# Block two of a feed-forward layer goes from a mix of eight and seven products to seven throughout, its weight sums supplied in another way

## The chip, the cores and the metric

The kernel runs on one core of one Trainium2 chip. The metric is device time in microseconds (us) of one launch; the time before is the median of three runs. The profile is that of one execution. Its times count from the first instruction of the span. PE is the matrix engine (PEld its weight loads), DVE the vector engine, ACT the scalar engine, POOL the GpSimd, and SP the engine whose queue issues most loads. Each engine runs its instructions in the order written and waits for others by semaphores.

## The reference

One decoder layer for 256 tokens of width 2048: a normalisation, one input projection, two groups of attention heads, an output projection, and then the feed-forward part, which alone is touched here:

```python
h = x + jnp.concatenate([gla_out, nsa_out], axis=-1) @ w_out
m = rms_norm(h, ffn_norm_g)
return h + (jax.nn.silu(m @ w_gate) * (m @ w_up)) @ w_down
```

`w_gate` and `w_up` are 2048 x 5632, `w_down` is 5632 x 2048, all float32.

## The kernel before

**Precision.** A float32 operand is kept as two parts: `hi`, a rounded copy in the matmul's input type, written by ACT (L661), and `lo`, what is left, `x - hi`, written by DVE (L662). One product of two operands is three matmuls: hi by hi, hi by lo, lo by hi.

**Blocks and pairs.** The 5632 columns are cut into eleven blocks of 512 (`f` = 0 to 10 in the code; "block one" to "block eleven" here, so block two is `f = 1`). In each block `gate_up` works through the 16 row tiles of the weights in eight pairs of two. Of a pair, the weights are four tiles of 128 x 512 (two of gate, two of up), and the tokens are two tiles of 128. Done plainly, a pair is eight products, 24 matmuls. Done in seven products, it is 21 matmuls, with four sums of the pair's weights and four sums of its tokens. The token sums are made once per pair (`pair_forms`); those of pairs 6 and 7 are made late (`late_forms`, during block two). `FIRST7` names the pairs that are done in seven in blocks one and two; from block three on all are.

**Where the weight sums come from.** There are three ways:
- *DVE*: one 128x1024 add and two 128x512 adds (L1229 to L1231).
- *DRAM sums* (`SUMS`): the four sums are made much earlier, in the attention part, by SP loads, DVE adds and POOL stores (`sum_rows`), kept in DRAM, and fetched by two POOL transfers of 512 KB (`fetch_sums`, L1172); the pair's own load is then 768 KB in place of 1 MB.
- *adding pair* (`HALVES`): two POOL transfers and a third that adds in flight make the first two sums in memory (`fetch_half`, L1182 to L1184); DVE makes the other two with two 128x512 adds. Its own load too is 768 KB.

In all of them the three plain tiles that are used (128x1536) and the four sums (two times 128x1024) are split by ACT and DVE into `ftwo` tiles, which a pair takes two of; a plain pair takes one of 128x2048. There are four `ftwo` tiles, four `fraw` tiles for the loads, and three `fsum` tiles, which hold weight sums and also the block's results on their way through the activation.

**After a block.** When the last seven-product pair is through, five operations (L1256 to L1260) put the product banks together; L1271 to L1275 add, apply the SiLU and multiply. `turn_act` then transposes the two result tiles on PE (L215), and splits them. `down` multiplies them with `w_down`: four chunks of 24 matmuls (L297), whose banks ACT seeds with the sum so far (L1310) and empties afterwards (L1322). `down` of a block stands behind the next block's pairs. In blocks three and later `turn_act` runs while the next block begins, in bank 8, which only plain pairs use otherwise; for block one it runs at the end of block two, in banks 1 and 5, since block two has plain pairs and needs bank 8.

**Order.** Instructions are put in order on each engine by a scheduler when the kernel is built. Loads are issued as soon as the tile that they fill is free.

Of the kernel before, what the change touches and what calls it, by code (L numbers as in the profile page):

```python
# [22 lines left out]
NFB = DFF // FB  # L23
# [14 lines left out]
def kernel(  # L38
# [989 lines left out]
    PAIRS7, FIRST7 = tuple(range(8)), {0: (0, 2, 4), 1: (0, 2, 3, 4, 5)}  # L1028
# [3 lines left out]
    HALVES = {f: (2, 6) if f < 8 else (2, 4, 6) for f in range(2, NFB)}  # L1032
# [4 lines left out]
    ORDER1 = (0,1,2,6,3,4,5,7)  # L1037
# [61 lines left out]
    SUMS = {f: (4, 7) if f < 8 else (7,) for f in range(2, NFB)}  # L1099
    SUMS[1] = (2, 3, 4, 5)  # L1100
# [87 lines left out]
    def gate_up(fb):  # L1188
# [12 lines left out]
        order, sevens = (ORDER0, ORDER1, ORDER)[min(fb, 2)], FIRST7.get(fb, PAIRS7)  # L1201
# [5 lines left out]
        if fb > 1:  # L1207
            urgent.append(turn_act(fb - 1, (8, 8)))
        for at, pair in enumerate(order):
            if fb > 1 and pair not in sevens:  # L1210
                drain(urgent)
# [42 lines left out]
            if pair == last7:  # L1254
                (q1, q7u), (u, q5u), (q57u, _) = ((t[:, 0], t[:, 1]) for t in (fw["sum"]([2, 512]) for _ in range(3)))
                act(q1, banks[1], AF.Copy)  # L1256
                TT(u, banks[6], q1, ALU.add)  # L1257
                TT(q5u, banks[5], u, ALU.subtract)
                TT(q7u, banks[7], u, ALU.add)
                TT(q57u, banks[5], q7u, ALU.subtract)  # L1260
                if fb == 1:
                    urgent.append(turn_act(0, (1, 5)))
                if fb:
                    seed(0, DOWN[min(fb - 1, 1)])
# [15 lines left out]
    def turn_act(fb, qs):  # L1280
# [4 lines left out]
        for t in range(NT):  # L1285
            ts = slice(t * P, (t + 1) * P)
            p = banks[qs[t]]
# [18 lines left out]
    DOWN = ((6, 7), (2, 3), (6, 7), (4, 8)), ((1, 6), (7, 5), (2, 3), (4, 1))  # L1306

    def seed(n, qs):
        for t in range(NT):
            last["seed", n] = nc.scalar.copy(banks[qs[n][t]], h_sb[n][:, t, :])  # L1310

    def down(f):
        ah, al = acts.pop(f)
        qs = DOWN[min(f, 1)]
        for n in range(4):
            bs = [banks[q] for q in qs[n]]
            ws = parts_of(load4([(w_down[0], 4 * f, 4, n * 512)]), last["seed", 0] if n == 2 and f else None)
            if n < 3 and (f or n != 1):
                seed(n + 1, qs)
# [3 lines left out]
            if n == 0 and not f:  # L1323
                seed(2, qs)
# [99 lines left out]
    for f in range(NFB):  # L1424
# [3 lines left out]
        if f:  # L1428
            drain(urgent)
            if f == NFB - 1:  # L1430
                urgent.append(turn_act(f, (8, 8)))
            drive([down(f - 1)], 3)
# [32 lines left out]
```

## Time and profile before

| | |
|---|---|
| median of three runs | 1095.1 us (1094.86 to 1095.49) |
| the profiled execution | 1095.91 us, its span 1094.2 us |
| busy share of the span | PE 99%, PEld 82%, DVE 90%, ACT 70%, POOL 12% |
| granted PE clock | 1.00 throughout |
| block one and two (`gate_up`) | 409.4 to 493.99 us; block two begins at 453.36 |
| `down` of block one | 493.99 to 516.41 us |
| block three, `down` of block two | 516.41 to 555.78, to 577.54 us |

The borders are the starts of the first matmuls, found by counting the matmuls of the trace along the program's order. The feed-forward part is 685 us of the span. A row of the windows view shows, for a stretch of time, how long each engine was busy and with how many instructions.

### The profile page before, as it was taken

Reading aid. Unit: us, or ns where it says so; the run is one execution under the profiler, and the core shown is the slowest. Engines: PE = TensorE matmul, PEld = TensorE weight load, DVE = VectorE, ACT = ScalarE, POOL = GpSimd, SP = SyncE. Lnnn points to the kernel's source line nnn. Section 1 sums busy time; section 2 is a strip of 40 time slices with the busy share of each in tenths; the row PEclk is TensorE's granted clock in tenths of the full one; section 3 lists DMA queues with packets and bytes.
Section 4 is the critical chain, followed back from the end, with each engine's and each line's share of the span. In section 5 each row is a group of like instructions: output and inputs, shape, how many; then the busy total and the mean of one; then the engine's idle time right before and its main releaser. Section 6 shows DMA issues by size and latency. Waiting matters only on the chain.

```text
span 1094.2 us, 14835 instructions
## 1 busy us (share of the span) xinstructions
PE 1088.2 (99%) x5256; PEld 895.3 (82%) x5256; DVE 988.4 (90%) x1316; ACT 764.7 (70%) x1060; POOL 129.2 (12%) x213
## 2 busy tenths in 40 slices
PE   9999999999999999999999999999999999999998
PEld 8888888987878877888888888888888887888877
DVE  6768879987799888997999999999999999999997
ACT  7745557555687586677686967777686877777695
POOL 4100001032110100010101011010101011110100
PEclk9999999999999999999999999999999999999999
DMA  7999978468876947696787969787797869788862
GB/s 278 357 356 350 398 251 295 166 232 287 308 274 252 342 153 287 216 336 208 250 278 221 299 200 302 246 266 236 261 288 236 280 207 288 227 279 255 247 231 78
DMA packets 135272, 287.76 MB, mean 263 GB/s; under 512 B 8135, under 2 KB 10219, under 8 KB 135197
## 3 DMA queue, kind: packets, MB, share of 16 engines
q1 hardware_dynamic: 112844, 218.17, 57.4%
q0 software_dynamic: 21744, 68.17, 20.4%
q8 instruction: 41, 0.67, 0.2%
q10 hardware_dynamic: 608, 0.47, 0.1%
q14 instruction: 35, 0.28, 0.1%
HBM read 263.71 MB, written 23.07 MB: 262 GB/s over the span
## 4 chain that ended last, share of the span: by engine, by line
PE 85%; DVE 6%; issue 3%; ACT 2%; DMA 2%; POOL 1%; SPq 0%; DVEq 0%; POOLq 0%; ACTq 0%
PE bank L297 41%; PE bank L1194 37%; PE bank L215 3%; PE bank L1339 2%; DVE lo L145 2%; PE bank L977 1%; DMA fraw<-in_w_up_dram 1%; DMA g<-in_w_up_dram 1%; POOL sm L218 1%; DMA sums<-g 1%; ACT g L912 1%; DVE ftwo L662 0%; DVE g L1115 0%; ACT hi L144 0%; PE bank L899 0%
## 5 line engine op out<-in xcount | busy, mean ns | idle before, releaser
L1194 PE MATMUL bank<-ftwo,g 128*128 128x512 f32 x1824 | 427.1, 393 | 0.5 <-ACT ftwo L661 0.2
L1194 PEld LDWEIGHTS bank<-ftwo,g 128*128 128x128 f32 x1824 | 337.2, 188 | 77.5 <-ACT ftwo L661 3.2
L297 PE MATMUL bank<-hi,g 128*128 128x512 f32 (+1 forms) x1088 | 320.9, 376 | 0.4 <-ACT g L912 0.4
L662 DVE TENSOR_TENSOR ftwo<-fraw,ftwo 128x1536 fp32r<-128x1536 f32 (+1 forms) x130 | 253.0, 1952 | 4.7 <-ACT ftwo L661 4.7
L661 ACT ACTIVATE ftwo<-fraw 128x1536 fp32r<-128x1536 f32 (+1 forms) x130 | 212.5, 1641 | 17.5 <-PE bank L1194 14.4
L297 PE MATMUL bank<-ftwo,g 128*128 128x512 f32 x960 | 221.6, 391 | 0.0
L297 PEld LDWEIGHTS bank<-hi,g 128*128 128x128 f32 x1088 | 191.5, 188 | 31.0 <-issue 1.0
L297 PEld LDWEIGHTS bank<-ftwo,g 128*128 128x128 f32 x960 | 179.3, 188 | 39.5 <-ACT bank L1310 1.2
L297 PE MATMUL bank<-lo,g 128*128 128x512 f32 (+3 forms) x544 | 193.0, 375 | 0.1
L144 ACT ACTIVATE hi<-raw 128x1024 fp32r<-128x1024 f32 (+3 forms) x124 | 130.5, 1059 | 82.8 <-PE bank L297 56.0
L145 DVE TENSOR_TENSOR lo<-raw,hi 128x1024 fp32r<-128x1024 f32 (+3 forms) x124 | 150.2, 1219 | 30.3 <-ACT hi L144 29.7
L661 ACT ACTIVATE ftwo<-fsum 128x1024 fp32r<-128x1024 f32 x118 | 121.9, 1054 | 70.6 <-DVE fsum L1229 53.6
L662 DVE TENSOR_TENSOR ftwo<-fsum,ftwo 128x1024 fp32r<-128x1024 f32 x118 | 142.0, 1221 | 13.7 <-ACT ftwo L661 13.7
L297 PEld LDWEIGHTS bank<-lo,g 128*128 128x128 f32 x544 | 98.2, 189 | 14.5 <-DVE lo L145 0.3
L661 ACT ACTIVATE ftwo<-g 128x1024 fp32r<-128x1024 f32 x46 | 48.7, 1059 | 35.8 <-PE bank L1194 23.3
L1322 ACT COPY g<-bank 128x512 f32<-128x512 f32 x80 | 45.6, 583 | 27.8 <-PE bank L297 26.4
L662 DVE TENSOR_TENSOR ftwo<-g,ftwo 128x1024 fp32r<-128x1024 f32 x46 | 56.2, 1221 | 2.2 <-ACT ftwo L661 2.2
L1119 POOL DMA_DIRECT2D sums<-g x40 | 21.8, 545 | 260.1 <-DVE g L1115 206.3
L1310 ACT COPY bank<-g 128x512 f32<-128x512 f32 x80 | 45.1, 589 | 7.6 <-DVE fsum L1257 6.2
L1229 DVE TENSOR_TENSOR fsum<-fraw 128x1024 f32<-128x1024 f32 x36 | 44.0, 1223 | 0.1
L215 PE MATMUL bank<-ident,g 128*128 128x128 f32 (+3 forms) x232 | 42.6, 277 | 0.6 <-ACT g L912 0.5
L1231 DVE TENSOR_TENSOR fsum<-fsum,fraw 128x512 f32<-128x512 f32 x60 | 41.4, 689 | 1.0
(251 smaller groups left out, 951.8 us busy)
## 6 DMA issues: line engine op xcount, KB each, us to landing
fraw<-in_w_gate_dram SPq DMA_DIRECT2D x86, 512.0 KB, 4.4
fraw<-in_w_down_dram SPq DMA_DIRECT2D x42, 1024.0 KB, 6.8
raw<-in_w_in_dram SPq DMA_DIRECT2D x36, 1024.0 KB, 6.1
fraw<-in_w_up_dram SPq DMA_DIRECT2D x45, 512.0 KB, 5.4
sums<-g POOLq DMA_DIRECT2D x40, 512.0 KB, 6.6
raw<-in_w_out_dram SPq DMA_DIRECT2D x16, 1024.0 KB, 8.5
g<-in_w_up_dram POOLq DMA_DIRECT2D x21, 512.0 KB, 7.6
fraw<-in_w_up_dram SPq DMA_DIRECT2D x41, 256.0 KB, 4.3
```

The source lines that it names most:

```text
L144: act(h[:, i:i + n], r[:, k + i:k + i + n], AF.Copy)
L145: last["d"] = TT(o[:, i:i + n], r[:, k + i:k + i + n], f32(h[:, i:i + n]), ALU.subtract)
L215: return nc.tensor.transpose(o, i, ident[:n, :n])
L297: last["mm"] = mm(bk[t], a[:, k, t * P:(t + 1) * P], ws[k][m][:, off:off + w], start=(first_ and k == 0 and i == 0), stop=(end and k == 3 ...
L661: act(hi, ps, AF.Copy)
L662: last["d"] = TT(lo, ps, f32(hi), ALU.subtract)
L1194: mm(banks[q], x, m, start=todo[q] == total[q], stop=todo[q] == 1)
L1229: TT(s1, r[:, 1:3], r[:, 3:4].to_broadcast([P, 2, 512]), ALU.add)
L1231: TT(s2[:, 1], s2[:, 0], r[:, 0], ALU.add)
L1310: last["seed", n] = nc.scalar.copy(banks[qs[n][t]], h_sb[n][:, t, :])
L1322: nc.scalar.copy(h_sb[n][:, t, :], bs[t])
L1339: mm(bk, u, m, start=(first and i == 0), stop=(end and i == 2), skip_group_check=onto)
```

## The change

Block two is done in seven products throughout: `FIRST7` loses its entry for it, and the order of its pairs becomes 0 to 7. Its DRAM sums are now those of the pairs 1, 3, 4, 6 and 7 (they were 2, 3, 4 and 5); the pairs 0, 2 and 5 have their sums made by DVE (before: pair 0 alone, while 1, 6 and 7 were plain and needed none). Block three (`f = 2`) gives up its DRAM sums of pair 4, which becomes a third adding pair, so that the number of stored sums stays at twenty pairs. Since bank 8 is now free in block two, `turn_act` of block one moves from the end of block two to its beginning, and `down` of block one takes its banks in the order that the later blocks have.

```diff
-    PAIRS7, FIRST7 = tuple(range(8)), {0: (0, 2, 4), 1: (0, 2, 3, 4, 5)}
+    PAIRS7, FIRST7 = tuple(range(8)), {0: (0, 2, 4)}
-    HALVES = {f: (2, 6) if f < 8 else (2, 4, 6) for f in range(2, NFB)}
+    HALVES = {f: (2, 6) if 2 < f < 8 else (2, 4, 6) for f in range(2, NFB)}
-    ORDER1 = (0,1,2,6,3,4,5,7)
-    SUMS = {f: (4, 7) if f < 8 else (7,) for f in range(2, NFB)}
-    SUMS[1] = (2, 3, 4, 5)
+    SUMS = {f: (4, 7) if 2 < f < 8 else (7,) for f in range(2, NFB)}
+    SUMS[1] = (1, 3, 4, 6, 7)
-        order, sevens = (ORDER0, ORDER1, ORDER)[min(fb, 2)], FIRST7.get(fb, PAIRS7)
+        order, sevens = (ORDER0, ORDER)[min(fb, 1)], FIRST7.get(fb, PAIRS7)
-        if fb > 1:
-            urgent.append(turn_act(fb - 1, (8, 8)))
+        if fb:
+            urgent.append(turn_act(fb - 1))
-                if fb == 1:
-                    urgent.append(turn_act(0, (1, 5)))
                 if fb:
-                    seed(0, DOWN[min(fb - 1, 1)])
+                    seed(0)
-    DOWN = ((6, 7), (2, 3), (6, 7), (4, 8)), ((1, 6), (7, 5), (2, 3), (4, 1))
+    DOWN = (1, 6), (7, 5), (2, 3), (4, 1)
```

**DVE, the last pairs of block two.** `fraw` is a load, `ftwo` a split tile, `fsum` and `g` hold sums. Before, pairs 4 and 5 (DRAM sums), then pair 7 (plain, 128x2048), then the first chunk of `down`:

```order
L662 TENSOR_TENSOR ftwo_4876<-fraw_4873,ftwo_4876 128x1536
L662 TENSOR_TENSOR ftwo_4888<-g_873_4833,ftwo_4888 128x1024
L662 TENSOR_TENSOR ftwo_4888<-fsum_4834,ftwo_4888 128x1024
L662 TENSOR_TENSOR ftwo_4908<-fraw_4905,ftwo_4908 128x1536
L662 TENSOR_TENSOR ftwo_4920<-g_878_4869,ftwo_4920 128x1024
L662 TENSOR_TENSOR ftwo_4920<-fsum_4870,ftwo_4920 128x1024
L662 TENSOR_TENSOR ftwo_4950<-fraw_4947,ftwo_4950 128x2048
L662 TENSOR_TENSOR ftwo_5001<-fraw_4999,ftwo_5001 128x2048
```

Now the end of pair 5 (sums by DVE), then pairs 6 and 7 (DRAM sums), then the first chunk of `down`:

```order
L1226 TENSOR_TENSOR g_888_4902<-fraw_4896 128x1024
L1227 TENSOR_TENSOR fsum_4903<-g_888_4902,fraw_4896 128x512
L1228 TENSOR_TENSOR fsum_4903<-fsum_4903,fraw_4896 128x512
L662 TENSOR_TENSOR ftwo_4916<-g_888_4902,ftwo_4916 128x1024
L662 TENSOR_TENSOR ftwo_4940<-fraw_4937,ftwo_4940 128x1536
L662 TENSOR_TENSOR ftwo_4916<-fsum_4903,ftwo_4916 128x1024
L662 TENSOR_TENSOR ftwo_4952<-g_884_4892,ftwo_4952 128x1024
L662 TENSOR_TENSOR ftwo_4952<-fsum_4893,ftwo_4952 128x1024
L662 TENSOR_TENSOR ftwo_4972<-fraw_4969,ftwo_4972 128x1536
L662 TENSOR_TENSOR ftwo_4975<-g_891_4933,ftwo_4975 128x1024
L662 TENSOR_TENSOR ftwo_4975<-fsum_4934,ftwo_4975 128x1024
L662 TENSOR_TENSOR ftwo_5020<-fraw_5018,ftwo_5020 128x2048
```

The last pair, for which one operation stood, now has three, and pair 5 has its three adds more. From the split of pair 0's load to the split of pair 7's last tile, DVE has 42 instructions before and 56 now.

**PE, the end of block two.** Before, pair 7 plain, with half of block one's transposes (L215) among it, and then `down` (L297):

```order
L1194 MATMUL bank_4386<-ftwo_4950,g_801_4337 128x512 x2
L1194 MATMUL bank_4386<-ftwo_4950,g_802_4338 128x512
L215 MATMUL bank_4464<-ident,fsum_4597 128x128 x2
L1194 MATMUL bank_4398<-ftwo_4950,g_801_4337 128x512 x2
L1194 MATMUL bank_4398<-ftwo_4950,g_802_4338 128x512
L297 MATMUL bank_4487<-ftwo_5001,g_891_4968 128x512 x2
```

Now pair 7 in seven products, from the first use of its third and fourth sums (bank_4487) on:

```order
L1193 MATMUL bank_4483<-ftwo_4975,g_882_4866 128x512 x3
L1193 MATMUL bank_4487<-ftwo_4975,g_882_4866 128x512 x2
L1193 MATMUL bank_4350<-ftwo_4972,g_801_4337 128x512 x2
L1193 MATMUL bank_4350<-ftwo_4972,g_802_4338 128x512
L1193 MATMUL bank_4369<-ftwo_4972,g_882_4866 128x512 x3
L1193 MATMUL bank_4386<-ftwo_4975,g_801_4337 128x512 x2
L1193 MATMUL bank_4386<-ftwo_4975,g_802_4338 128x512
L297 MATMUL bank_4464<-ftwo_5020,g_860_4713 128x512 x2
```

The two matmuls into bank_4487 need what DVE writes last for pair 7; with them 11 matmuls are left to the block's end. Block two has 168 matmuls now, and had 177; its transposes are all of block one's eight, and were four.

**POOL, the fetches for block two.** The stored tiles are named by block and pair (`sums_1_4` is `f = 1`, pair 4; two per pair). Before:

```order
L1172 DMA g_858_4715<-sums_1_2_749 128x1024 [waits DMASW2_49,PE_49]
L1172 DMA fsum_4716<-sums_1_2_750 128x1024 [waits DMASW3_49,DMASW1_49,DVE_49]
L1172 DMA fsum_4800<-sums_1_3_836 128x1024 [waits DMASW4_49,DVE_49]
L1172 DMA fsum_4834<-sums_1_4_927 128x1024 [waits DMASW5_49,DMASW3_49,DVE_49]
L1172 DMA g_869_4799<-sums_1_3_835 128x1024 [waits DMASW6_49]
L1172 DMA g_873_4833<-sums_1_4_926 128x1024 [waits DMASW7_49,DMASW2_49]
L1172 DMA g_878_4869<-sums_1_5_1044 128x1024 [waits DMASW0_49,DVE_49,PE_49]
L1172 DMA fsum_4870<-sums_1_5_1045 128x1024 [waits DMASW4_49,DVE_49]
```

Now:

```order
L1171 DMA g_853_4678<-sums_1_1_749 128x1024 [waits DMASW2_49,PE_49]
L1171 DMA fsum_4679<-sums_1_1_750 128x1024 [waits DMASW3_49,DVE_49]
L1171 DMA g_865_4765<-sums_1_3_835 128x1024 [waits DMASW4_49]
L1171 DMA fsum_4766<-sums_1_3_836 128x1024 [waits DMASW5_49,DVE_49,PE_49]
L1171 DMA fsum_4816<-sums_1_4_927 128x1024 [waits DMASW6_49,DMASW1_49,DVE_49]
L1171 DMA fsum_4893<-sums_1_6_1045 128x1024 [waits DMASW7_49,DMASW3_49,DVE_49]
L1171 DMA g_874_4815<-sums_1_4_926 128x1024 [waits DMASW0_49]
L1171 DMA g_884_4892<-sums_1_6_1044 128x1024 [waits DMASW0_49,DVE_49]
L1171 DMA fsum_4934<-sums_1_7_1178 128x1024 [waits DMASW6_49,DMASW2_49]
L1171 DMA g_891_4933<-sums_1_7_1177 128x1024 [waits DMASW4_49,DVE_49]
```

There are ten fetches where there were eight, and pair 4's first sums now stand behind pair 6's second sums, which wait for DVE to free an `fsum` tile. From the second pair of block four on, all engines have the same instructions in the same order as before.

More of the change, by code (lines that the diff above doesn't have):

```diff
@@ L1206, in gate_up @@
         total = dict(todo)
-        if fb > 1:
-            urgent.append(turn_act(fb - 1, (8, 8)))
+        if fb:
+            urgent.append(turn_act(fb - 1))
         for at, pair in enumerate(order):
-            if fb > 1 and pair not in sevens:
-                drain(urgent)
             if fb == 0 and at == len(OLD):
@@ L1278, with turn_act @@
     hidden, acts = {}, {}
-    def turn_act(fb, qs):
+    def turn_act(fb):
         for _ in range(2):
@@ L1286, in turn_act @@
             ts = slice(t * P, (t + 1) * P)
-            p = banks[qs[t]]
+            p = banks[8]
             for j in range(4):
@@ L1300, in turn_act, with seed @@
                 pair_forms(8 + pair, v, f)
-    DOWN = ((6, 7), (2, 3), (6, 7), (4, 8)), ((1, 6), (7, 5), (2, 3), (4, 1))
-    def seed(n, qs):
+    DOWN = (1, 6), (7, 5), (2, 3), (4, 1)
+    def seed(n):
         for t in range(NT):
-            last["seed", n] = nc.scalar.copy(banks[qs[n][t]], h_sb[n][:, t, :])
+            last["seed", n] = nc.scalar.copy(banks[DOWN[n][t]], h_sb[n][:, t, :])
     def down(f):
         ah, al = acts.pop(f)
-        qs = DOWN[min(f, 1)]
         for n in range(4):
[L1316 to L1319, printed above, removed]
+            bs = [banks[q] for q in DOWN[n]]
+            ws = parts_of(load4([(w_down[0], 4 * f, 4, n * 512)]), last["seed", 0] if n == 2 else None)
+            if n < 3:
+                seed(n + 1)
             yield from chunk([bs], ah, al, ws, False, True, onto=True)
@@ L1322, in down @@
                 nc.scalar.copy(h_sb[n][:, t, :], bs[t])
-            if n == 0 and not f:
-                seed(2, qs)
     def down_last():
@@ L1430 @@
             if f == NFB - 1:
-                urgent.append(turn_act(f, (8, 8)))
+                urgent.append(turn_act(f))
             drive([down(f - 1)], 3)
```

## The prediction

> **What bounds the kernel now.** I read the page's busy shares first, then the chain of waits, then the windows view cut at the borders of the blocks, and last the timeline of DVE inside block two.
>
> ```profile
> PE 1088.2 (99%) x5256; PEld 895.3 (82%) x5256; DVE 988.4 (90%) x1316; ACT 764.7 (70%) x1060; POOL 129.2 (12%) x213
> ```
>
> PE is full, and DVE follows close behind. The chain of waits (start, length, what) says how PE spends its time in the feed-forward part:
>
> ```profile
> 436.45 55.18 PE bank L1194 x242
> ...
> 555.94 21.76 PE bank L297 x96
> ```
>
> A chunk of `down` runs at 21.76 / 96 = 0.2267 us for a matmul, with nothing between. PE sets the end there, and a matmul less is worth 0.2267 us, as long as DVE can split the weights in time. Whether it can is told by the stretches (start:end, length, then busy time and instructions of PE, PEld, DVE, ACT, POOL, clock, DMA share, GB/s):
>
> ```profile
> 453.36:493.99 40.63, 40.63 (x182) 33.57 (x181) 37.83 (x42) 29.00 (x27) 5.99 (x10) 1.00 0.94 322
> 493.99:516.41 22.42, 22.42 (x102) 18.25 (x101) 19.10 (x19) 14.79 (x21) 0.00 (x0) 1.00 0.54 179
> 516.41:555.78 39.37, 39.37 (x178) 32.02 (x176) 37.53 (x35) 29.05 (x29) 6.53 (x10) 1.00 0.79 264
> 555.78:577.54 21.76, 21.76 (x98) 18.02 (x96) 20.95 (x20) 16.65 (x22) 0.29 (x1) 1.00 0.83 247
> 577.54:617.00 39.46, 39.46 (x178) 32.00 (x176) 38.59 (x37) 29.15 (x29) 6.82 (x10) 1.00 0.79 265
> 519.32:554.99 35.67, 35.67 (x161) 28.94 (x160) 35.60 (x34) 26.09 (x24) 5.74 (x10) 1.00 0.77 256
> ```
>
> The rows are block two, `down` of block one, block three, `down` of block two, block four, and the last nine tenths of block three. The last row decides the argument: a block in seven products throughout keeps DVE busy for 35.60 of 35.67 us. Such blocks are at the limit of both engines, and PE does not wait only because DVE enters them with a lead. A block and a `down` like the fifth and the fourth row need 38.59 + 20.95 = 59.5 us of DVE in 61.2 us. Block two is the slack one, and this slack is what the change spends.
>
> **The change, part by part: PE.** Block two loses 9 matmuls (three pairs of 24 become 21): 9 x 0.2267 = 2.04 us. Four transposes come in from `down`. A block of 168 matmuls and eight transposes that waits for nothing is the third row, 39.37 us; a `down` without transposes is the fourth, 21.76. For PE alone, the two stretches would fall from 40.63 + 22.42 to 39.37 + 21.76, by 1.92 us.
>
> **DVE in block two.** The timeline of DVE (start, duration, and in brackets the idle time before and its releaser), from the split of pair 0's load to the split of pair 7's:
>
> ```profile
> 443.58 1.75 DVE L662 TENSOR_TENSOR ftwo<-fraw,ftwo 128x1536 fp32r<-128x1536 f32 x1
> ...
> 448.87 1.23 DVE L662 TENSOR_TENSOR ftwo<-g,ftwo 128x1024 fp32r<-128x1024 f32 x1 [0.60 <-ACT ftwo L661]
> 450.01 0.68 DVE L1271 TENSOR_TENSOR fsum<-bank,fsum 128x512 f32<-128x512 f32 x1
> 450.84 0.69 DVE L1274 TENSOR_TENSOR fsum<-bank,fsum 128x512 f32<-128x512 f32 x1
> 451.45 2.28 DVE L662 TENSOR_TENSOR ftwo<-fraw,ftwo 128x2048 fp32r<-128x2048 f32 x1
> 453.64 0.75 DVE L1275 SCALAR_TENSOR_TENSOR fsum<-fsum,rf,fsum 128x512 f32<-128x512 f32 x1
> ...
> 455.50 0.69 DVE L1230 TENSOR_TENSOR fsum<-g,fraw 128x512 f32<-128x512 f32 x1
> 456.10 0.75 DVE L1275 SCALAR_TENSOR_TENSOR fsum<-fsum,rf,fsum 128x512 f32<-128x512 f32 x1
> ...
> 457.97 1.76 DVE L662 TENSOR_TENSOR ftwo<-fraw,ftwo 128x1536 fp32r<-128x1536 f32 x1
> 459.64 1.23 DVE L662 TENSOR_TENSOR ftwo<-fsum,ftwo 128x1024 fp32r<-128x1024 f32 x1
> 460.77 0.29 DVE L1046 TENSOR_TENSOR g<-g 128x128 f32<-128x128 f32 x1
> ...
> 472.60 1.23 DVE L662 TENSOR_TENSOR ftwo<-g,ftwo 128x1024 fp32r<-128x1024 f32 x1 [1.04 <-ACT ftwo L661]
> ...
> 482.73 2.29 DVE L662 TENSOR_TENSOR ftwo<-fraw,ftwo 128x2048 fp32r<-128x2048 f32 x1 [0.53 <-ACT ftwo L661]
> ```
>
> The stretch ends at 482.73 + 2.29 = 485.02, and as a window it is:
>
> ```profile
> 443.58:485.02 41.44, 41.44 (x184) 34.29 (x183) 38.82 (x43) 27.01 (x23) 5.78 (x10) 1.00 0.82 293
> ```
>
> 38.82 us of work, 2.62 idle. What the order of the changed kernel adds there: three splits of 128x2048 go, three of 128x1536 come; eight operations of 128x1024 (six splits of sums, two first adds of pairs 2 and 5); six of 128x512 (four second adds, and two for block one's transposes, which stood behind the block). From one start to the next in the rows above, they take 2.19, 1.67, 1.13 and 0.60 us. That makes 3 x 1.67 - 3 x 2.19 + 8 x 1.13 + 6 x 0.60 = 11.1 us.
>
> So DVE has 38.8 + 11.1 = 49.9 us to do before pair 7 is split, and begins, as before, at 443.58. It ends at 493.5 plus its idle time. Of that, 0.75 us (the gaps before 448.87 and 450.84) lies ahead of the first changed instruction and stays: not before 494.3. With the 2.62 of the old stretch it is 496.1. I take 2.0 idle, 495.5: an engine that is behind waits for less, but the added splits have ACT rows of their own ahead of them, and PE now frees `ftwo` tiles later.
>
> Behind that last split PE has 11 matmuls of the block, 2.5 us. Block two ends at 498.0, where it ended at 493.99: **+4.0 us** (+2.8 to +4.6). PE alone would be there at 453.36 + 39.37 = 492.7, so that PE stands for some 5 us. The cover that is gone is DVE's lead: pair 0 was split at 445.33, eight microseconds ahead of its first use, and this is in the sum.
>
> [...]
>
> **`down` of block one.** It was 22.42, four transposes in it. Now it is 21.76 for PE alone; but DVE comes late to it. What that costs is shown by the blocks with three adding pairs, nine and ten, beside block eight with two:
>
> ```profile
> 822.38:861.76 39.38, 39.38 (x177) 31.90 (x176) 38.52 (x37) 29.06 (x29) 6.65 (x10) 1.00 0.80 265
> 861.76:883.52 21.76, 21.76 (x97) 18.02 (x96) 20.99 (x20) 16.69 (x22) 0.16 (x1) 1.00 0.81 245
> 883.52:923.06 39.54, 39.54 (x178) 31.85 (x176) 38.68 (x37) 28.91 (x28) 6.93 (x10) 1.00 0.79 252
> 923.06:945.24 22.18, 22.18 (x98) 17.86 (x96) 22.08 (x22) 17.17 (x23) 1.23 (x1) 1.00 0.85 262
> 945.24:984.82 39.58, 39.58 (x178) 31.72 (x176) 38.69 (x37) 28.89 (x28) 6.93 (x10) 1.00 0.80 252
> ```
>
> With the third adding pair, block nine takes 39.54 for 39.38 and the `down` in which DVE arrives late 22.18 for 21.76. I take 22.1 here: **-0.3** (-0.66 to -0.2).
>
> **Block three and after.** Its third adding pair costs DVE two more 128x512 adds, 1.2 us. DVE enters some 3 us later than before, but so does PE, and before DVE idled there:
>
> ```profile
> 506.71 1.76 DVE L662 TENSOR_TENSOR ftwo<-fraw,ftwo 128x1536 fp32r<-128x1536 f32 x1 [1.86 <-ACT ftwo L661]
> ...
> 518.18 2.36 DVE L662 TENSOR_TENSOR ftwo<-fsum,ftwo 128x1024 fp32r<-128x1024 f32 x2 [2.89 <-ACT ftwo L661]
> ```
>
> These 4.75 us repay the debt, so that the loss is not made twice. Block three becomes a block nine: **+0.15** (0 to +0.5), its `down` **+0.4** (0 to +0.5), and block four, by block ten beside block four, **+0.1** (0 to +0.3). Further on the order is the same, and the shift stays. Early on, twenty stored pairs are made in the same slots: 0.
>
> **The sum**, on the profiled execution's span: 4.0 - 0.3 + 0.15 + 0.4 + 0.1 = +4.35 us, 1094.2 to 1098.5. That execution took 1095.91, 0.8 above the median of 1095.1; what lies around the span does not change. On the median: **1099.4 us**. With the ends of all terms: 1097.2 to 1101.0.
>
> **The rivals.**
> - *A, faster: DVE's lead covers its added work.* Then PE's saving stands, 1095.1 - 1.9 = 1093.2. It is decided by the time at which DVE ends pair 7: it would have to be 492.7 - 2.5 = 490.2, and DVE would have 46.6 us for 49.9 of work. For it speaks that PE waits for next to nothing in the feed-forward part now; against it the row 519.32:554.99, in which DVE has nothing left to give.
> - *B, no difference: the debt is smaller*, because the rows pack tighter than 11.1 or the scheduler has found work to shift. With the lower bounds of all terms and another 1 us it is 1096.2.
> - *C, slower still: a fetch is late.* In the old order the first sums of pair 3 went out at 464.76 and ACT had to wait for them until 471.51, 6.75 us later; that is the gap of 1.04 at 472.60:
>
> ```profile
> 464.76 1.04 POOL L1172 DMA_DIRECT2D g<-sums  x2
> 471.51 1.06 ACT L661 ACTIVATE ftwo<-g 128x1024 fp32r<-128x1024 f32 x1 [1.02 <-DMA g<-sums]
> ```
>
>   Now pair 4's first sums stand behind a fetch that waits for DVE's last use of pair 2's sums, the 27th of the 56 instructions; added up in the same way, with 0.7 idle, it ends at about 470.3. Two issues later, 471.3, plus 6.75 is 478.1, and ACT's split ends at 479.2. DVE wants it for its 42nd, by the same sum at 479.0. Each microsecond more is one at the end, since DVE has no slack: with 2 us, 1101.4.
> - *D, the added rows do not overlap*, because each waits for the one ahead (sum, sum of the sum, split). Then they cost the durations of the rows above, 3 x 1.76 - 3 x 2.28 + 8 x 1.23 + 6 x 0.69 = 12.4 in place of 11.1: 1100.7. In pair 5 the two second adds now follow each other directly, but in the pairs 0 and 2 other work stands between.
> - *That the change does not do what it says*: the order has 168 matmuls in block two and no plain pair, so I give it nothing.
>
> **Chances.** The forecast 0.66, A 0.05, B 0.10, C 0.13, D 0.06. A measurement of this kernel tells about 0.2%, 2.2 us, from no change; that is 1097.3 upwards. The forecast (nearly all of it), C and D lie above, B inside: faster 0.05, same 0.10, slower 0.85. The range leaves out A and the far end of C: 1096.2 to 1101.8.
>
> **What would show it.** The changed kernel's first matmul of `down` behind block two at about 498, with the stretch from 453.36 about 44.6 long; in it, DVE busy for over 95% and PE standing for about 5 us, released by the splits (DVE and ACT `ftwo`), most of it in pairs 4 to 7. `down` of block one near 22.1, block three near 39.5 and its `down` near 22.2; from block five on the old lengths. If block two is 39.4 long, A is right and the reckoning of DVE is wrong. If PE's or ACT's gaps there end with `g<-sums` or `fsum<-sums` transfers, it is C. If DVE is through with pair 7 before 494.3, a row is dearer in my sum than in the kernel.

## The result: six and a half microseconds slower

The changed kernel takes **1101.81 us** (median of 6 runs, 1101.4 to 1102.49), the kernel before, run beside it, 1095.17 (1094.63 to 1097.34). The ratio is 1.0059, with a 95% interval from 1.0046 to 1.0072. The direction of the forecast holds; its 1099.4 was 2.4 us too low. The time lies at the very end of the range (1101.8), and beyond 1101.0, where the ends of all its terms stood. The profiled execution took 1101.46, its span is 1099.8.

The page's busy shares of the changed kernel:

```profile
PE 1090.1 (99%) x5247; PEld 893.6 (81%) x5247; DVE 999.1 (91%) x1329; ACT 770.0 (70%) x1066; POOL 131.6 (12%) x216
```

PE lost nine matmuls and is busy for more time than before (1088.2). In part that is how the profile counts: the ends of matmuls are modelled, and those beside a stop count longer (below, two of them beside a stop have 0.73 us, where 2 x 0.2267 is 0.45). In part some matmuls have become slower. The windows view of the changed kernel, cut at the same borders as before: block two, `down` of block one, block three, its `down`, and last DVE's stretch in block two, from the split of pair 0's load to the end of pair 7's last split:

```profile
452.53:499.69 47.16, 43.31 (x177) 32.52 (x176) 44.34 (x50) 31.50 (x31) 7.04 (x12) 0.96 0.79 272
499.69:521.47 21.78, 21.78 (x97) 18.02 (x96) 20.98 (x20) 16.70 (x22) 0.00 (x0) 1.00 0.79 243
521.47:561.00 39.53, 39.53 (x178) 31.71 (x176) 38.66 (x37) 28.90 (x28) 7.10 (x11) 1.00 0.82 252
561.00:583.21 22.21, 22.21 (x98) 17.87 (x97) 22.11 (x22) 17.20 (x23) 1.05 (x1) 1.00 0.84 262
442.76:496.19 53.43, 49.58 (x205) 37.73 (x204) 50.25 (x57) 32.61 (x31) 5.79 (x11) 0.97 0.73 253
```

Block two grew from 40.63 to 47.16 us, by 6.5; its `down` lost 0.64, block three gained 0.16, the `down` behind it 0.45; block four took 39.45 for 39.46. Together that is 6.49 us; the span grew by 5.6 only because block two happened to begin 0.83 us earlier in this execution. So the whole loss lies in block two. PE works 43.31 of its 47.16 us, at a mean clock of 0.96. Before, the chain of waits ran through PE alone here. Now it is (start, length, what):

```profile
460.32 5.66 DMA fsum<-sums
...
469.57 0.52 POOL fsum L1171
470.09 7.36 DMA g<-sums
...
486.13 13.72 PE bank L1193 x52
```

The two DMA rows are fetches of stored sums, for pair 3 and for pair 4. The last row is PE without a stop, but 52 matmuls should take 52 x 0.2267 = 11.8 us, not 13.7. The granted clock accounts for 1.6 of these 1.9 us (8 matmuls at 0.425 us each in place of 0.2267). The windows of the changed kernel just ahead of the slow matmuls, and over them:

```profile
476.00:486.13 10.13, 6.56 (x24) 3.56 (x22) 9.03 (x13) 5.55 (x6) 1.04 (x2) 1.00 0.60 211
486.20:489.60 3.40, 3.40 (x8) 2.63 (x9) 3.40 (x3) 3.40 (x4) 0.53 (x1) 0.51 0.98 312
```

PE stood for a third of ten microseconds, and then 8 matmuls took 3.40 us, 0.425 each, at a granted clock of 0.51. DVE's timeline has two waits late in the block, before the splits of the first sums of pairs 4 and 7:

```profile
478.56 1.23 DVE L662 TENSOR_TENSOR ftwo<-g,ftwo 128x1024 fp32r<-128x1024 f32 x1 [0.99 <-ACT ftwo L661]
...
493.82 1.23 DVE L662 TENSOR_TENSOR ftwo<-g,ftwo 128x1024 fp32r<-128x1024 f32 x1 [0.88 <-ACT ftwo L661]
494.97 1.22 DVE L662 TENSOR_TENSOR ftwo<-fsum,ftwo 128x1024 fp32r<-128x1024 f32 x1
```

ACT, which splits first, had waited for the transfers there (ACT's timeline):

```profile
477.47 1.06 ACT L661 ACTIVATE ftwo<-g 128x1024 fp32r<-128x1024 f32 x1 [3.85 <-DMA g<-sums]
492.73 1.06 ACT L661 ACTIVATE ftwo<-g 128x1024 fp32r<-128x1024 f32 x1 [2.43 <-DMA g<-sums]
493.70 1.04 ACT L661 ACTIVATE ftwo<-fsum 128x1024 fp32r<-128x1024 f32 x1
```

The trace leaves three candidates for the 2.5 us that block two has beyond the forecast: DVE's added work was dearer than reckoned, the fetches were late, or the half clock cost time. The experiments tell them apart.

### The profile page after: what moved, and what is told of

The parts are those of the page before. It is cut to its first block, busy times and chain, and to the rows that moved or that the text cites. A ratio compares the mean times of both kernels' runs of the same rounds, so it can differ in the third digit from the quotient of the medians.

```text
span 1099.8 us, 14848 instructions
## 1 busy us (share of the span) xinstructions
PE 1090.1 (99%) x5247; PEld 893.6 (81%) x5247; DVE 999.1 (91%) x1329; ACT 770.0 (70%) x1066; POOL 131.6 (12%) x216
## 4 chain that ended last, share of the span: by engine, by line
PE 88%; DVE 4%; ACT 3%; issue 3%; DMA 1%; POOL 0%; DVEq 0%; ACTq 0%; POOLq 0%
PE bank L297 44%; PE bank L1193 36%; PE bank L215 3%; PE bank L1331 2%; DVE lo L145 1%; PE bank L977 1%; ACT hi L144 1%; DMA g<-sums 1%; ACT g L912 1%; DMA fsum<-sums 1%; ACT ftwo L661 0%; PE bank L603 0%; PE bank L899 0%; PE bank L805 0%; DVE g L1114 0%
## 5 line engine op out<-in xcount | busy, mean ns | idle before, releaser
L297 PE MATMUL bank<-hi,g 128*128 128x512 f32 (+1 forms) x1088 | 321.0, 376 | 0.8 <-ACT g L912 0.4
L297 PE MATMUL bank<-ftwo,g 128*128 128x512 f32 x960 | 221.6, 390 | 0.0
L297 PEld LDWEIGHTS bank<-hi,g 128*128 128x128 f32 x1088 | 191.6, 188 | 31.1 <-issue 1.0
L297 PEld LDWEIGHTS bank<-ftwo,g 128*128 128x128 f32 x960 | 179.4, 188 | 39.7 <-DVE ftwo L662 1.6
L297 PE MATMUL bank<-lo,g 128*128 128x512 f32 (+3 forms) x544 | 193.0, 375 | 0.1
L661 ACT ACTIVATE ftwo<-fsum 128x1024 fp32r<-128x1024 f32 x121 | 125.2, 1054 | 73.8 <-DVE fsum L1226 56.6
L662 DVE TENSOR_TENSOR ftwo<-fsum,ftwo 128x1024 fp32r<-128x1024 f32 x121 | 145.5, 1218 | 11.5 <-ACT ftwo L661 11.4
L297 PEld LDWEIGHTS bank<-lo,g 128*128 128x128 f32 x544 | 98.3, 189 | 14.6 <-DVE lo L145 0.3
L661 ACT ACTIVATE ftwo<-g 128x1024 fp32r<-128x1024 f32 x49 | 51.8, 1058 | 45.2 <-PE bank L1193 22.2
L662 DVE TENSOR_TENSOR ftwo<-g,ftwo 128x1024 fp32r<-128x1024 f32 x49 | 59.7, 1218 | 2.9 <-ACT ftwo L661 2.9
L215 PE MATMUL bank<-ident,g 128*128 128x128 f32 (+3 forms) x232 | 42.5, 277 | 0.2 <-ACT g L912 0.2
```

The costliest lines, as they stand in the source:

```text
L215: return nc.tensor.transpose(o, i, ident[:n, :n])
L297: last["mm"] = mm(bk[t], a[:, k, t * P:(t + 1) * P], ws[k][m][:, off:off + w], start=(first_ and k == 0 and i == 0), stop=(end and k == 3 ...
L661: act(hi, ps, AF.Copy)
L662: last["d"] = TT(lo, ps, f32(hi), ALU.subtract)
```

## The experiments

In the profiled executions the part ahead of block two varies by about 2 us from one to another (a load of block one's up-weights lands earlier or later: ACT waited 0.79 us for it in the changed kernel, 2.67 and 3.01 in two of the runs below), and the medians with it. So I measure block two as a **stretch**: from the start of DVE's split of pair 0's first sums (448.87 in the kernel before, 448.04 in the changed one) to PE's first matmul of the `down` behind it. Before and change, as windows:

```profile
448.87:493.99 45.12, 45.12 (x202) 37.28 (x201) 42.18 (x45) 32.79 (x30) 5.99 (x10) 1.00 0.85 291
```

```profile
448.04:499.69 51.65, 47.80 (x197) 36.24 (x196) 48.69 (x54) 34.85 (x34) 7.04 (x12) 0.97 0.72 249
```

45.12 has become 51.65: again 6.5 us. Two pairs of executions have the same work in the stretch, before and the third adding pair alone, and change and block two alone; each pair agrees within 0.01 us. The clock in the table is the granted clock over the stretch in the profiled execution. All runs:

| kernel | median, us | ratio to before (95%) | stretch, us | clock | `down` behind it, us |
|---|---|---|---|---|---|
| before | 1095.17 | 1 | 45.12 | 1.00 | 22.42 |
| change | 1101.81 | 1.0059 (1.0046 to 1.0072) | 51.65 | 0.97 | 21.78 |
| third adding pair alone | 1096.98 | 1.0008 (0.9996 to 1.0020) | 45.12 | 1.00 | 23.02 |
| block two alone | 1103.22 | 1.0070 (1.0057 to 1.0083) | 51.64 | 1.00 | 21.76 |
| filled gaps | 1101.96 | 1.0059 (1.0045 to 1.0072) | 51.23 | 1.00 | 21.75 |
| two fetches less | 1103.91 | 1.0068 (1.0056 to 1.0081) | 51.70 | 0.97 | 23.13 |
| filled gaps, two fetches less | 1102.76 | 1.0065 (1.0053 to 1.0077) | 49.86 | 1.00 | 24.77 |
| 4.5 us of DVE less | 1101.31 | 1.0052 (1.0038 to 1.0066) | 50.06 | 0.97 | 21.76 |
| fetches in other tiles | 1102.13 | 1.0056 (1.0042 to 1.0070) | 50.83 | 0.97 | 21.76 |
| other tiles, 4.5 us of DVE less | 1100.02 | 1.0038 (1.0025 to 1.0050) | 48.96 | 1.00 | 21.76 |
| 4.5 us of DVE more | 1104.73 | 1.0080 (1.0066 to 1.0094) | 54.95 | 0.97 | 21.91 |
| all forms early | 1100.36 | 1.0038 (1.0026 to 1.0050) | 46.17 | 1.00 | 21.81 |
| forms early and half pairs | 1111.66 | 1.0136 (1.0122 to 1.0150) | - | - | 21.76 |
| before, 4.5 us of DVE more | 1098.45 | 1.0011 (0.9999 to 1.0023) | 45.25 | 1.00 | 23.31 |

The ratios are each to runs of the kernel before on the same chip (1095.2 to 1096.7 us there), so rows are compared by their ratios. By these intervals no variant of block two but the one with half pairs is clear of the change; what the variants show rests on the stretch, which is one execution each. The kernel with half pairs has other rows at the stretch's start, so it has no number for it.

### The two parts of the change

Block three's edit alone, on the kernel before:

```diff
-    HALVES = {f: (2, 6) if f < 8 else (2, 4, 6) for f in range(2, NFB)}
+    HALVES = {f: (2, 6) if 2 < f < 8 else (2, 4, 6) for f in range(2, NFB)}
...
-    SUMS = {f: (4, 7) if f < 8 else (7,) for f in range(2, NFB)}
+    SUMS = {f: (4, 7) if 2 < f < 8 else (7,) for f in range(2, NFB)}
```

> The kernel before with one part of the change: block three's third adding pair (with one stored pair fewer there); block two is as before. My theory, that block two makes nearly all of the loss, expects the stretch of block three at 39.4 to 39.6 us for 39.37, its down at 21.8 to 22.2 for 21.76, together 0.2 to 0.6 us more than before: 1095.4 to 1095.8. The rival, that the loss is spread over the blocks and comes from DVE having one more pair to add in block three (2 us of its work, 0.3 to 0.5% of nothing hidden), expects 2 us or more: 1097.2 or above.

Measured: block three and its `down` as windows:

```profile
517.28:556.76 39.48, 39.48 (x177) 31.75 (x176) 37.63 (x35) 28.85 (x28) 6.96 (x10) 1.00 0.80 252
556.76:578.95 22.19, 22.19 (x97) 17.87 (x96) 22.09 (x22) 17.18 (x23) 1.22 (x1) 1.00 0.86 262
```

0.11 and 0.43 us more than before, 0.54 together. By these windows the rival is out. The whole time does not decide it: the median is above what I expected, and its interval holds no difference at all as well as the rival's 2 us. (The `down` ahead of it, which this edit does not touch, was 0.6 longer here; ACT waited 1.40 us in it for a load of `w_down`, which it did not before. Why that load was late is open.) Now the changed kernel with the same two lines put back as they were:

> The changed kernel with block three as it was (two adding pairs, its pair 4 stored as sums); block two has all eight pairs in seven products. My theory: block two keeps its 47.2 us, block three and its down go back to 39.4 + 21.8, so 0.6 us less than the changed kernel, 1101.2. The twenty-first stored pair would cost more than that only if the early part had no room for it; then 1102 or above. The rival, that block three's debt makes the loss, expects 1098 or below.

```profile
450.05:501.69 51.64, 46.45 (x198) 35.06 (x196) 48.72 (x54) 34.62 (x34) 7.07 (x12) 1.00 0.73 249
...
523.45:562.87 39.42, 39.42 (x177) 31.98 (x176) 38.56 (x37) 29.11 (x29) 6.39 (x10) 1.00 0.79 264
562.87:584.63 21.76, 21.76 (x97) 18.02 (x96) 20.96 (x20) 16.66 (x22) 0.45 (x1) 1.00 0.82 246
```

The blocks came out as expected: the stretch keeps its length, block three and `down` return to 39.42 and 21.76. But the median did not fall to 1101.2; with its interval the ratio overlaps that of the change. In the profiled execution the feed-forward part began at 411.00, two microseconds later than in the changed kernel. That shows no price of the twenty-first stored pair: among the variants below that leave the part ahead as it is in the changed kernel, it began anywhere from 408.99 to 410.79. One thing more is to be seen: here the clock stayed at 1.00 and the stretch is as long as in the changed kernel, where it fell to half. The half clock alone did not make the loss. The chain of waits shows what stood there in its place, a fetch and the matmuls behind it:

```profile
488.93 5.68 DMA g<-sums
...
496.77 5.08 PE bank L1193 x21
```

Other executions agree. Of the six of the changed kernel, five have a mean clock of 0.998 over the span (3.4 us at half clock in 1100 lower it by 0.0015), and one has 1.000; that one took 1101.61 us, 0.2 below the median.

### The half clock and the late fetch

Sixteen matmuls more, at the places in pairs 3 to 5 where PE stood, into a bank nobody reads then:

```diff
+    DUMMY = {3: 2, 4: 3, 5: 3}
...
+                    if fb == 1 and at in DUMMY and q in (1, 7):
+                        for _ in range(DUMMY[at]):
+                            mm(banks[8], forms[0][:, 0, 0], hT_h[0][:, 0:2, :].rearrange("p a b -> p (a b)"), start=True, stop=True)
```

> The changed kernel with 16 further matmuls of 128x512 in block two, two to three at each place in pairs 3, 4 and 5 at which PE stands (their result, in a bank not in use there, is never read). They are 16 x 0.227 = 3.6 us of PE work, put where PE stood for about 5. My theory, that the clock fell to half after these gaps and that the slow matmuls put PE about 1 us behind DVE at the end of the block, expects the clock at 1.00 throughout block two, 11 matmuls behind DVE's last split in 2.5 us instead of 3.5, and the block 0.3 to 1.2 us shorter in spite of more work: 1100.6 to 1101.5. Rival one, that the half clock was free because PE waits for DVE anyway, expects no gain, 1101.8, or up to 1 us more where the added matmuls do not fit in the gaps. Rival two, that the clock falls for another reason than the gaps, expects a clock below 1.00 in block two here as well.

The clock stayed at 1.00 (all five executions have a mean of 0.999 or 1.000 over the span), which speaks against rival two: with the gaps filled it fell in none of the five. The stretch fell by 0.4 us, to 51.23, in spite of 3.6 us more work; that is the low end of what I expected, and the median does not show it. The chain of waits of this kernel says what held it now:

```profile
487.51 5.21 DMA g<-sums
...
493.79 1.05 ACT ftwo L661
...
494.89 5.10 PE bank L1194 x21
```

The fetch for pair 7 landed late, ACT split the first and then the second sums, and only then did PE do its last 21 matmuls, in 5.10 us: in PE's order the first matmul with the second sums stands 21 ahead of the block's end. In the changed kernel PE came to this point at 494.93 (499.69 less 21 x 0.2267), ACT at 494.74 (493.70 + 1.04): two limits of one height. The next kernel takes away the other one: pairs 4 and 7 use the tiles fetched for pairs 3 and 6.

```diff
-        if (fb, pair) in row_sums:
+        if fb == 1 and pair in (4, 7):
+            fetched[fb, pair] = fetched[fb, pair - 1]
+        elif (fb, pair) in row_sums:
```

> The changed kernel without the fetches of the stored sums of pairs 4 and 7 of block two: their products use the tiles fetched for pairs 3 and 6, so the result differs there; all splits and products stay. My theory, that an engine without slack pays each wait in full, expects DVE's gaps of 0.99 and 0.88 us before the splits of these sums to go and the block to be 1.5 to 2.0 us shorter, 1099.8 to 1100.3 (down to 1099.0 if the clock no longer falls). The rival, that these waits only stand where DVE would have waited for a free tile or for ACT anyway, expects gaps of the same size with another releaser and no change: 1101.5 to 1102.

Neither theory had it right: DVE's two gaps went (one of 1.00 us came, before the split of pair 1's second sums), and the stretch stayed at 51.70. The chain of waits, and the windows of the stretch and of the `down` behind it:

```profile
487.46 13.71 PE bank L1195 x52
```

```profile
449.31:501.01 51.70, 47.34 (x198) 36.47 (x196) 49.44 (x54) 35.15 (x35) 4.93 (x8) 0.97 0.64 208
501.01:524.14 23.13, 22.28 (x97) 17.86 (x96) 20.29 (x20) 16.02 (x21) 0.00 (x0) 1.00 0.65 228
```

The same 52 matmuls again take 13.71 us without a stop, at a mean clock of 0.97 over the stretch: now the half clock sets the end. Both edits together:

> The changed kernel with both of the last two edits at once: the 16 further matmuls that fill PE's gaps, and no fetch for pairs 4 and 7 of block two (the result differs there). By itself neither made block two shorter. My theory now: two limits of nearly the same height stand above DVE's own at the end of the block, the late fetch for pair 7 (the end is ACT's split of pair 7's second sums plus 21 matmuls, 4.95 us) and the PE time lost to the half clock after the gaps; each run removed one and met the other. With both gone DVE's work sets the end, 2.5 us behind its last split: block two 1.5 to 2.0 us shorter than the changed kernel's, 45.2 to 45.7 us for 47.2, on the same chip about 1.8 us below the run with filled gaps alone. The rival, that the end of the block hangs on something else (the order of PE's last 21 matmuls, or the added matmuls themselves), expects no gain here either: 47 us or more.

```profile
449.31:499.17 49.86, 48.30 (x214) 38.54 (x212) 48.32 (x54) 34.29 (x34) 4.95 (x8) 1.00 0.64 211
499.17:523.94 24.77, 22.29 (x97) 17.86 (x96) 21.17 (x20) 16.89 (x22) 0.00 (x0) 1.00 0.68 222
```

```profile
487.23 12.10 PE bank L1196 x52
...
504.80 0.13 ACT ftwo L661
```

The stretch is 1.8 us shorter than in the changed kernel, as expected, and 1.6 of it is in the 52 matmuls: 12.10 us for 13.71 (8 x 0.2 = 1.6). So the half clock cost 1.8 us where the two fetches were out of the way (51.70 to 49.86), and the fetches 1.4 where the clock was (51.23 to 49.86); each hid behind the other, and taking one away gained 0.4 us or nothing. What sets the 49.86 is DVE's work in part only. DVE is busy for 97% of it, but so is PE (48.30 us, 3.6 of them the added matmuls); the chain still has one fetch at the block's start (6.21 us), then goes by turns through ACT, PE and DVE to DVE's first add for pair 5, and from there through ACT's split and PE's 52 matmuls.

And yet the median did not fall: `down` took 24.77 us for 21.78. The chain comes there to a split of ACT at 504.80. The run with two fetches less has the same place 0.2 later, as a wait for a load of `down` weights (timelines of POOL, of SP's queue and of ACT in that kernel):

```profile
493.46 1.23 POOL L1185 DMA_DIRECT2D g<-in_w_up_dram  x1 [4.63 <-issue]
```

```profile
494.30 0.37 SPq L1141 DMA_DIRECT2D fraw<-in_w_down_dram  x1
```

```profile
505.01 1.92 ACT L661 ACTIVATE ftwo<-fraw 128x2048 fp32r<-128x2048 f32 x1 [2.44 <-DMA fraw<-in_w_down_dram]
```

In the changed kernel the adding transfer goes out later (POOL's timeline):

```profile
497.86 1.25 POOL L1183 DMA_DIRECT2D g<-in_w_up_dram  x1 [6.35 <-issue]
```

With two fetches gone from POOL's queue, the adding transfer for block three goes out at 493.46, just ahead of the fourth load for `down`. ACT could begin with that load 10.7 us after its issue; in the changed kernel none of the four took longer than 7.8 us to land. That the adding transfer slowed it is my reading of the order and the times; no run put that transfer alone elsewhere.

### Is DVE's work the limit?

In pairs 2 and 5 the low part of the split sums is left out, four DVE operations of 128x1024:

```diff
-                        ws = parts_of2(s1, s2)
+                        ws = parts_of2(s1, s2, fb == 1 and pair in (2, 5))
```

> The changed kernel without DVE's splits of the sums of pairs 2 and 5 of block two (their products use the high part twice, so the low part is left out there); that is four operations of 128x1024 less, 4 x 1.13 = 4.5 us of DVE. My theory, that DVE has no slack in the block and everything that is late there (the fetch for pair 7, PE's gaps) hangs on it, expects block two 3.5 to 4.7 us shorter, 42.5 to 43.7 us, and the kernel at 1097.2 to 1098.3. The rival, that the fetches and the half clock set the block's end by themselves, expects 2 us or less: 1099.8 or above.

The stretch fell by 1.6 us only: a miss for my theory, and the rival's number. DVE's timeline and the chain of waits show where the rest went:

```profile
480.44 1.23 DVE L662 TENSOR_TENSOR ftwo<-g,ftwo 128x1024 fp32r<-128x1024 f32 x1 [3.31 <-ACT ftwo L661]
```

```profile
470.67 8.66 DMA g<-sums
...
480.46 19.11 PE bank L1197 x75
```

DVE, early by 2.3 us, stood 3.31 us for pair 4's first sums in place of 0.99. That fetch went out 21.3 us after the stretch's start (22.1 in the changed kernel) and took 8.7 us (7.4). It hardly moved with DVE's work. The clock fell here too (0.97 over the stretch): the 75 matmuls of the last row took 19.11 us, where 75 x 0.2267 is 17.0, and they stand behind that fetch without a stop. So this run meets both of the other limits and does not say how much of the block is DVE's own work. Two kernels move this fetch. In the first, the second sums of pairs 3 and 4 go to general tiles, so that fewer fetches wait for the three tiles for sums:

```diff
-            to = fetched[fb, pair] = g4([2, 512]), fw["sum"]([2, 512])
+            to = fetched[fb, pair] = g4([2, 512]), (g4 if fb == 1 and pair in (3, 4) else fw["sum"])([2, 512])
```

> The changed kernel with the stored second sums of pairs 3 and 4 of block two fetched into general 4 KB tiles instead of the three tiles for sums; DVE's work and the work of PE stay. My theory: in the changed kernel the first sums of pair 4 stand on POOL's queue behind a fetch of second sums (for pair 6) that waits for a tile for sums, go out 27.3 us after DVE's split of pair 0's load and land 34.7 us after it, 1 us after DVE could use them. With tiles free earlier they go out 2 to 5 us earlier, DVE's gap of 0.99 us goes, and block one and two together take 0.5 to 1.5 us less than the changed kernel's 90.7: 89.2 to 90.2; no more, since DVE's own work is then the limit. Rival: the fetch is not what holds the block, 90.5 or more.

Block one's load was late in this execution (ACT waited 3.01 us for it, 0.79 in the changed kernel). So block one and two together, 92.0 us, say nothing; the stretch is 50.83, 0.8 less. The size is what was expected (the clock fell here too, to 0.97 over the stretch), the way to it is not: DVE's gap before pair 4's sums is gone, but the fetch went out no earlier (POOL's timeline):

```profile
473.44 0.53 POOL L1171 DMA_DIRECT2D g<-sums  x1 [9.46 <-DVE g L1047]
```

That is 23.3 us after the start; it now waits for DVE's token forms to free a general tile, and landed within 4.2 us. With the low part of pairs 2 and 5 left out as well, the dose of less DVE work:

> The last edit together with the dose of less DVE work (no DVE splits of the sums of pairs 2 and 5 in block two, 4.5 us; the low part of these weights is left out). With the dose alone, block one and two came down by 1.3 us only, to 89.4, because DVE then stood 3.3 us for pair 4's first sums. My theory, two limits of nearly the same height, DVE's work and the fetch of pair 4, expects that with both lowered the 4.5 us come through, but for what other fetches and PE leave: 85.5 to 87.5 us for block one and two. The rival, that DVE's work was never the limit, expects the gain of the tiles alone, 89 us or more.

```profile
480.33 1.23 DVE L662 TENSOR_TENSOR ftwo<-g,ftwo 128x1024 fp32r<-128x1024 f32 x1 [2.22 <-ACT ftwo L661]
```

The stretch is 48.96, 2.7 less than in the changed kernel where 3.2 to 5.2 were expected: DVE still stands 2.22 us for the same fetch. (Block one and two together are 89.8 us, the rival's number; but a late load in block one, for which ACT waited 2.67 us, is in that sum.) The clock stayed at 1.00 in this execution, so part of the 2.7 may be the clock's. What the dose gives where no fetch is late was not tried. The other direction, the same four splits made twice:

```diff
+            if twice:
+                TT(lo[:, 2 * i:2 * i + 2], v, f32(hi[:, 2 * i:2 * i + 2]), ALU.subtract)
```

> The changed kernel with DVE's splits of the sums of pairs 2 and 5 of block two made twice, with the same result: four operations of 128x1024 more, 4 x 1.13 = 4.5 us of DVE, two of them ahead of pair 4's first sums, two behind. If DVE's work is a limit in both halves of the block, block one and two become 3.5 to 5.0 us longer than 90.7: 94.2 to 95.7, and the kernel 1105.3 to 1106.8. If the fetch of pair 4 is the limit of the first half by itself, its 2.3 us are hidden in part and the block grows by 2.3 to 3.3.

The stretch as a window:

```profile
450.00:504.95 54.95, 49.12 (x197) 35.72 (x196) 52.35 (x57) 34.59 (x33) 7.06 (x12) 0.97 0.70 236
```

The stretch grew by 3.3 us for 4.5 of work: the dose was hidden in part. DVE no longer waits for pair 4's first sums, as the second of the two cases has it; by its size the run stands at the border of the two (block one and two together are 94.2 us, 3.5 more). The growth is not all DVE's: the fetch for pair 7 is late again, by 1.19 us for DVE, and PE stands 0.56 us ahead of `down`. And the same dose in the kernel before:

> The kernel before, with DVE's splits of the sums of pairs 2 and 5 of block two made twice, with the same result: four operations of 128x1024, 4 x 1.13 = 4.5 us of DVE, put into the block with the old order. In the changed kernel the same dose made the block 3.3 us longer. My theory, that block two was the slack block and the first microseconds of the change's added DVE work were covered (by idle time of 2.6 us in DVE's stretch and by its lead), expects 0 to 0.8 us more for block one and two, 84.6 to 85.4 us, and with the shift of DVE's debt into the next stretch 1095.7 to 1097.5 for the kernel on a chip where before takes 1096. The rival, that DVE was at its limit in the old block too, expects 2.5 to 4.5 us more: 87.1 or above.

```profile
450.62:495.87 45.25, 45.25 (x202) 37.21 (x201) 43.55 (x48) 33.45 (x31) 5.99 (x10) 1.00 0.77 273
495.87:519.18 23.31, 22.99 (x102) 18.10 (x100) 21.88 (x20) 14.06 (x18) 0.00 (x0) 1.00 0.60 203
```

There 4.5 us of DVE cost 0.1 us in the block, in which PE never stands, and 0.9 in the `down` behind it: the old block was the slack one, as the forecast had it. (The late load made block one 1.7 us longer in this execution, so the sum with it, 86.4, misses the expected number; the median, 1098.45, is above it as well.)

### Moving DVE's work out

```diff
-    EARLY7 = (0,1,2,3,4,5)
+    EARLY7 = (0,1,2,3,4,5,6,7)
```

> The changed kernel with the token forms of the last two pairs made ahead of the feed-forward part, as those of the other six, instead of in block two: about 4.7 us of DVE work leave block two (18 operations) and are done in the attention part's last product, where DVE is busy for 84 to 91% of PE's time. My theory expects block two 3.5 to 4.7 us shorter, 42.5 to 43.7 us, and the part before it 0 to 2 us longer: 1097.2 to 1100.3. The rival, that the early part has no room either, expects the loss to be moved there: 1101 or above.

```profile
451.48:497.65 46.17, 44.58 (x198) 35.75 (x197) 44.80 (x42) 33.34 (x32) 7.08 (x12) 1.00 0.80 278
410.43:451.48 41.05, 39.16 (x172) 30.83 (x171) 36.27 (x44) 26.27 (x31) 2.27 (x4) 1.00 0.68 250
```

The stretch fell by 5.5 us, more than the 3.5 to 4.7 expected, and DVE is busy for 97% of it. The clock stayed at 1.00, so part of the gain may be the clock's. The fetch for pair 4 is early here too (ACT's timeline):

```profile
475.66 1.06 ACT L661 ACTIVATE ftwo<-g 128x1024 fp32r<-128x1024 f32 x1 [1.95 <-DMA g<-sums]
```

ACT has it 24.2 us after the stretch's start, in place of 29.4 in the changed kernel. So the edit lowers both limits, DVE's work and the fetch; that the forms' tiles are what the fetch got is likely (the fetch waited for them in the run with other tiles) and not shown. Two microseconds went back into block one (second row, 41.05 us for 39.05 in the changed kernel), of which PE stands for 1.9. Last, this and adding transfers for pairs 2 and 5:

```diff
+    HALVES[1] = (2, 5)
```

> As the kernel with all forms early, and pairs 2 and 5 of block two get their first sums by adding transfers, as blocks three to eleven do, which takes another two operations of 128x1024, 2.3 us, from DVE. My theory: DVE's work in the stretch of block two is then 50.2 - 4.7 - 2.3 = 43.2 us, and the block comes to 40.0 to 42.0 us, near the 39.5 of the blocks after it: 1094.5 to 1098. If DVE is not what holds the block, or if six more transfers on POOL's queue make the fetches of the stored sums later still, it does not come below the kernel with forms early alone.

The slowest of all, far beyond what I expected. The chain of waits:

```profile
479.20 4.86 DMA g<-in_w_up_dram
...
485.60 8.13 DMA g<-in_w_up_dram
...
496.20 14.99 PE bank L1194 x53
```

The adding transfers share POOL's queue with ten fetches, and DVE and PE stand for one that takes 8.1 us. Behind it the clock seems to have fallen again: 53 matmuls take 14.99 us, where 53 x 0.2267 is 12.0, and the mean clock over the span is 0.995 (0.998 in the changed kernel). None of the variants comes below the kernel before.

## Why the prediction was right, and by how much it was off

- **The whole.** The direction was right, and the mechanism too: DVE's added work outlasts PE's saving, in block two. The size was not. The ends of all terms reach 1101.0 (added up again, they make 1100.8), and 1101.81 lies beyond; that it still lies at the end of the range comes from the room left there for rival C, not from the sum.
- **Block two, +4.0 forecast, +6.5 measured.** This is the term that was mis-sized. It was made of DVE's work, its idle time and a tail. *Work*: 49.9 us forecast, 50.25 measured, so the rows from the old block carried; the rival by which the added rows do not overlap is out. *Idle*: 2.0 forecast, 3.2 measured (53.43 less 50.25), with the waits of 0.99 and 0.88 for the fetches of pairs 4 and 7. *Tail*: 11 matmuls, 2.5 us, behind DVE's last split; it was 499.69 less 496.19, 3.5 us. 0.35 + 1.2 + 1.0 is the 2.5 us that were missing.
- **What the tail missed.** I counted from DVE's last split, but PE waits earlier for ACT's split of the same sums, 21 matmuls before the end, and with a late fetch that comes last. And I took PE's rate as fixed, while the standing that the change caused itself was followed by 3.4 us at half the clock. With both out of the way (filled gaps, two fetches less) the stretch was 49.86; the forecast's 498.0 is 49.1 us after its start. So the sum is right within 0.7 us for a block without these two, and lies 1.8 us beneath that with them. That DVE by itself makes the 49.86 is not shown, since PE is as busy there.
- **Rival C, the late fetch, came true in part.** It put ACT's end of pair 4's split at 479.2 against DVE's 479.0, on the clock of the old execution; measured, 0.8 earlier on the whole, were 478.53 and 477.57. So the wait was 1.0 us where I had 0.2; the second one, 0.88 us for pair 7, C did not name. Its 1101.4 (with 2 us late) is closer to 1101.81 than my forecast, and 0.13 was too little for it. That a microsecond late is one at the end was shown only in part: two late microseconds went and the end stayed, since the half clock was as late.
- **The cover.** That block two was slack and the change spends this slack was right: 4.5 us of DVE cost 0.1 us in the old block (and 0.9 in the `down` behind it) and 3.3 in the new one.
- **The rest.** `down` -0.3 forecast, -0.64 measured (the end of its range: DVE was not late there); block three +0.15 and +0.16; its `down` +0.4 and +0.45; block four +0.1 and 0. Block three's edit by itself gave the same 0.1 and 0.4. That "the loss is not made twice" holds.
- **What I had said would show it**: the first matmul of `down` at about 498 came at 499.69; DVE is busy for 94% of block two (44.34 of 47.16 us), not for over 95; PE's row leaves 3.85 us of standing (47.16 less 43.31) instead of 5, but matmuls beside a stop count longer, and against an unhindered block PE lost 47.16 less 39.37, 7.8 us, some 1.8 of them in slow matmuls and 6 at the stops; the releasers are ACT's and DVE's splits, nearly all of it in pairs 4 and 5, within the forecast's pairs 4 to 7; the `g<-sums` rows in the chain are those I had named for C.

Open is how much of the stretch DVE's work alone would set (with no late fetch, the clock at 1.00 and no matmuls added), and whether the adding transfer is what slowed the load in `down`.

## What to carry to other kernels

When a change fills an engine's slack, the engine's own work may be only the lowest of the new limits: look at what its slack was hiding, here fetches whose tiles come free late, and size each as a limit of its own. If an experiment takes a suspect away and nothing moves, that does not clear it; look at whether the chain of waits now ends in another one, and take both away. For the tail of a block count the matmuls behind the last thing PE waits for, whichever engine makes it, in PE's own order.

## What the hardware showed that I had not expected

**Short stops, half clock.** The granted clock fell to 0.51 for 3.4 us (8 matmuls in 3.40 us) after ten microseconds in which PE was busy for 6.56 of 10.13, and no single stop was longer than 1.35 us (PE's timeline of the changed kernel):

```profile
484.75 0.73 PE L1193 MATMUL bank<-ftwo,g 128*128 128x512 f32 x2 [1.35 <-ACT ftwo L661]
```

In the run with block two alone PE was busy for 6.98 of 10.60 us ahead of the same place, and the clock stayed at 1.00 (windows of that kernel):

```profile
478.00:488.60 10.60, 6.98 (x25) 3.86 (x23) 9.46 (x13) 5.53 (x6) 1.05 (x2) 1.00 0.65 216
488.60:492.00 3.40, 3.37 (x15) 2.75 (x16) 3.40 (x4) 3.40 (x4) 0.53 (x1) 1.00 0.94 306
```

The longest stop there was 1.37 us. So nearly the same stops came with the half clock in one execution and without it in the other. One and the same kernel went both ways: of the six executions of the changed kernel five have a mean clock of 0.998 over the span and one has 1.000; of the five with block two alone three have 0.997 or 0.998 and two 1.000. With the gaps filled all five stayed at 0.999 or 1.000; with two fetches less besides, one of five had 0.998. What brings the clock down, and why it stayed down for 3.4 us, no run shows.

**Fetch times.** The fetches of 512 KB of stored sums that the changed kernel issued from 450 to 493 us landed after (us):

```profile
DMA to landing us min/median/max: 3.5/5.7/7.4
```

In the run with 4.5 us of DVE less one took 8.66 us (row above). The 6.75 of the old block was no constant; what makes one fetch slower than another, no run isolates.
